# One ring of 8 KB buffers for all weights, and part of the second feed-forward's operand sums made ahead in DRAM

## The chip, the cores and the metric

The kernel runs on one core of one Trainium2 chip, as one launch. The metric is the device time of that launch in microseconds (us); a median over several runs is compared. Five engines work beside each other on the core, each through its own list of instructions, strictly in order: PE (matrix products), DVE (elementwise on vectors), ACT (elementwise, with function tables), POOL and SP. DMAs are issued from SP's queue, some from POOL's and ACT's.

## The reference

One encoder layer on 256 tokens of width 2048, all in float32. What matters here are its two feed-forward blocks, at the start and at the end:

```python
def swiglu(h, w_up, w_down):
    gate, up = jnp.split(h @ w_up, 2, axis=-1)
    return (jax.nn.silu(gate) * up) @ w_down
...
x = x + 0.5 * swiglu(rms_norm(x, ffn1_norm[l]), ffn1_w_up[l], ffn1_w_down[l])
# a gated recurrence, an RG-LRU branch, gates and two projections; then cross-attention
x = x + 0.5 * swiglu(rms_norm(x, ffn2_norm[l]), ffn2_w_up[l], ffn2_w_down[l])
return rms_norm(x, final_norm)
```

The hidden width is 5632, so `w_up` is 2048 x 11264 and `w_down` 5632 x 2048.

## The kernel before

**Precision.** The large products take their operands as `float32r`, each split into a high part `h` (a copy by ACT into that type) and a low part `l` (the difference `raw - h`, by DVE), and each product is made of three matmuls: h·h, l·h and h·l. For every weight piece of 1 MB (128 x 2048 float32, 8 KB in a partition) there is therefore a DMA into `raw`, one pass of ACT and one of DVE before PE can use it.

**Feed-forward.** Each of the two (`ffn1`, `ffn2`) goes through 11 groups `g` of 512 hidden columns. A group has eight up pieces `p` (`wu[g, p]`: two row blocks of the model width, each with 512 gate and 512 up columns), and four down pieces (`wd`) that stand between the groups. `PRODUCTS` names the ways to multiply an up piece with the activations of two token blocks (a 2 x 2 by 2 x 2 block product). "plain" and "mixed" use eight products of blocks, so 8 x 3 = 24 matmuls of 512 columns. "fast" uses seven, so 21 matmuls, in the manner of Strassen; for it four sums of the weight blocks (`td`) are made first, and these are split too, into `th` and `tl`. `ffn_order` says which pieces are of which kind: group 0 is plain; in groups 1 and 2 the even pieces are mixed and the odd ones fast; from g = 3 on only p = 6 is mixed. A down piece takes 24 matmuls.

**Relief for DVE.** Some pieces are of the kind "added" (`begin_added`): ACT writes -h to `l`, and a DMA from POOL's queue adds `raw` (tile `own`) to it, so DVE has no part in it. These are the mixed piece p = 6 of each group from g = 3 on and 16 of the down pieces, in both feed-forwards.

**Buffers.** The 8 KB tiles lie in rings of their own: 3 `raw`, 3 `h`, 3 `l` for the whole program, and within the feed-forwards 3 `wide` (for `td`, `tl`, the eviction tile `ev` and `junk`) and one `own`: 13 in all.

**Order.** Operations are recorded in the order of the code and then arranged by a planner (`Flow.arrange`): it keeps a due time for each operation, prices of the operations and the rings' free buffers, and it writes out for every engine a list in which the instructions stand. The chip follows that list. Between the feed-forwards lies what is called the middle here: 194 pieces, all plain, with the recurrences and the attention beside them.

**Transposes.** When a group's hidden columns are ready, `turn` transposes them on PE (tile names `vt,ev`), two times four transposes, and splits them into `hidop` for the down products.

Of the kernel before, what the change touches and what calls it, by code (L numbers as in the profile page):

```python
# [14 lines left out]
P = 128  # L15
T = 256
# [26 lines left out]
def ffn_order():  # L43

    out, down = [("plain", 0, p) for p in range(8)], [("down", 0, 1, c, 0) for c in range(4)]
    for g in range(1, NG):  # L50
        if g < 3:
            out += [(("mixed", "fast")[p % 2], g, p) for p in (0, 1, 2, 3, 5, 4, 7, 6)]
# [40 lines left out]
class Buffer(View):  # L93


    def __init__(self, ring, shape, dt, name):
        grain = shape[1] if "space" in ring.pool.kw else 1 if shape[1] <= 128 else 32
        super().__init__(self, np.arange(shape[1]) // grain)
        self.ring, self.shape, self.dt, self.name = ring, shape, dt, name
        self.at = self.index = None  # L100
        n = -(-shape[1] // grain)
        self.writer, self.readers = [None] * n, [set() for _ in range(n)]
        self.users = []
        self.left = 0


class Ring:
    def __init__(self, pool, tag, bufs):
        self.pool, self.tag, self.bufs = pool, tag, bufs
        self.takers = []  # L110
        self.spare = bufs if bufs < 8 else bufs // 4
        self.reset()

    def reset(self):
        self.free = [(0.0, i, None) for i in range(self.bufs)]
        self.head, self.taken = 0, set()

    def when(self, op):

        if not self.free or self.takers[self.head] is not op and len(self.free) <= self.spare:  # L120
            return 1e18
        return min(self.free)[0]

    def take(self, op):
        f = min(self.free)
        self.free.remove(f)
# [3 lines left out]
        return f  # L130


class Pool:
# [5 lines left out]
    def tile(self, shape, dt, name, tag=None, bufs=None):  # L139
        tag = tag or name  # L140
        if tag not in self.rings:
            self.rings[tag] = Ring(self, tag, bufs or self.bufs)
        return Buffer(self.rings[tag], shape, dt, name)
# [20 lines left out]
AHEAD, BACKLOG = 30, 3  # L164
# [3 lines left out]
class Flow:  # L168


    def __init__(self, tc):
        self.tc, self.ops, self.pools, self.scopes = tc, [], [], 0
        nc = tc.nc
        self.queues = [Queue(self, n, e) for n, e in (
            ("PE", nc.tensor), ("DVE", nc.vector), ("ACT", nc.scalar), ("SP", nc.sync), ("POOL", nc.gpsimd))]

# [4 lines left out]
    def record(self, queue, method, args, kw):  # L181
# [28 lines left out]
        for v in {v.tile for v in ins + outs}:  # L210
# [5 lines left out]
            s = v.ring.pool.scope  # L216
# [7 lines left out]
    def price(self, op, method, args, kw, outs):  # L224
# [8 lines left out]
        elif q == "PE":  # L233
            op.busy += n / 2400 + 0.0134 if not op.turn else 0.021 if n <= 32 else 0.07 + n * 1.05e-3
# [25 lines left out]
    def arrange(self):  # L260
        from heapq import heappop, heappush
# [15 lines left out]
        for p in self.pools:  # L277
            for r in p.rings.values():
                r.reset()
        live = [0] * (self.scopes + 1)  # L280
# [8 lines left out]
        dma = reached = 0.0  # L289
        events = []  # L290
        for t in {t for op in ops for t in op.tiles}:
            t.left, t.ends = len(t.users), 0.0
        for op in ops:
            if not op.waits:
                cand[op.queue.name].append(op)
# [4 lines left out]
        opened = 0  # L300
        while events:
            t, e = heappop(events)
            if free[e] > t + 1e-9:
                continue
            best, soon = None, 1e18
            for op in cand[e]:
                r = op.ready
                if op.scope is not None and any(live[:op.scope]) and any(x.ring.pool.scope is not None for x in op.takes):
                    continue
                for x in op.takes:  # L310
                    r = max(r, x.ring.when(op))
                if op.nominal > reached + AHEAD:
                    r = 1e18
                if op.moved:
                    r = max(r, dma - BACKLOG)
                if r <= t + 1e-9:
                    if best is None or op.due < best.due:
                        best = op
# [23 lines left out]
            for x in op.takes:  # L342
                f = x.ring.take(op)
                woken.update(names)
                x.index = f[1]
                x.before = f[2]
                if f[2] is not None:
                    for u in f[2].users:
                        if u is not op:
                            u.extra.append(op)  # L350
            if op.scope is not None:
                live[op.scope] -= 1
                if not live[op.scope]:
                    woken.update(names)
            for x in op.tiles:
                x.left -= 1
                x.ends = max(x.ends, op.end)
                if not x.left:
                    x.ring.free.append((x.ends, x.index, x))
                    woken.update(names)  # L360
            for s in op.after:
# [9 lines left out]
                if not s.waits:  # L371
                    cand[s.queue.name].append(s)
# [9 lines left out]
    def emit(self):  # L382
# [13 lines left out]
        for _ in range(3):  # L396
            self.arrange()
        with ExitStack() as outer:
# [3 lines left out]
            for op in self.sequence:  # L402
                if op.scope is not None and op.scope != scope and op.takes:
                    if inner is not None:
                        inner.close()
                    inner, scope = ExitStack(), op.scope
                    open_pools(inner, scope, reuse_waits="tile")
                for x in op.takes:
                    x.at = x.ring.pool.at.tile(x.shape, x.dt, name=x.name, tag=f"{x.ring.tag}{x.index}")
# [6 lines left out]
def block_kernel(tc: tile.TileContext, xT, xin, memT, vec, gfin, bgate, lruw, wu1, wd1, win, wv,  # L416
# [6 lines left out]
    rawp = pool("raw", 3)  # L423
    hp = pool("h", 3)
    lp = pool("l", 3)
    slots = pool("slots", 24)
    small = pool("small", 2)
    psum = pool("psum", 8, space=bass.MemoryType.PSUM)
    scoped = {}

    @contextmanager
    def scope(**pools):
        for name, bufs in pools.items():
            scoped[name] = pool(name, bufs, flow.scopes)
        flow.scopes += 1
        yield
        scoped.clear()

# [36 lines left out]
    def split_tiles():  # L475
        return hp.tile([P, 2048], F32R, name="h", tag="h"), lp.tile([P, 2048], F32R, name="l", tag="l")
# [3 lines left out]
    orders = dict.fromkeys(("ffn1", "ffn2"), ffn_order())  # L480

    def plan_ffn(name, wu, wd):
        for e in orders[name]:
# [4 lines left out]
            if e[0] == "down" and 0 < e[1] < NG - 2 and (e[3] + e[4] - e[1]) % 2 == 0:  # L488
# [9 lines left out]
    plan_ffn("ffn1", wu1, wd1)  # L498
    for hf in range(2):
# [12 lines left out]
    for name, w in (("mv", wvm), ("o", wo)):  # L512
        for g in range(4):
            plan_rows(name, w, g)
    plan_ffn("ffn2", wu2, wd2)
# [4 lines left out]
    def weights(*key):  # L520
        while plan and len(ahead) < 2:
            i = next(planned)
            k, src, kind = plan.pop(0)
            if i < len(head):
# [4 lines left out]
            if i in rest:  # L529
                rest[i]()  # L530
        k, w = ahead.pop(0)
        assert k == key, (k, key)
        return w

    begun = []

    def begin_added(src):

        raw = scoped["own"].tile([P, 2048], F32, name="own", tag="own")
        l = lp.tile([P, 2048], F32R, name="l", tag="l")  # L540
# [5 lines left out]
    def prepare(src, kind, cuts=1):  # L546

        if kind == "added":
            raw, l = begun.pop(0)
            h = hp.tile([P, 2048], F32R, name="h", tag="h")  # L550
            done["high"] = act.activation(h, raw, ACT.Copy).ins
            return h, l
        raw = rawp.tile([P, 2048], F32, name="raw", tag="raw")
        n = 2048 // cuts
        if kind == "plain":
# [4 lines left out]
            return h, l  # L560
        sp.dma_start(raw, src)
        td = scoped["wide"].tile([P, 2048], F32, name="td", tag="wide")
# [6 lines left out]
        th = hp.tile([P, 2048], F32R, name="h", tag="h")  # L569
        tl = scoped["wide"].tile([P, 2048], F32R, name="tl", tag="wide")  # L570
# [120 lines left out]
    FFN_POOLS = dict(wide=3, own=1, third=1)  # L691

    class TokenSquares:
# [5 lines left out]
        def add(self, c, ts=range(2)):  # L699
            for t in ts:  # L700
                if "wide" in scoped:
                    junk = scoped["wide"].tile([P, 2048], F32, name="junk", tag="wide")[:, :512]
# [53 lines left out]
    BOTH = [0, 2, 4]  # L756
    xd = []

    def operand_pairs(src, gain, q, xg, out):

        for a in src:
# [7 lines left out]
            less = None if i else (h[:, 512:768], l[:, 512:768])  # L769
            if 2 * q + i in BOTH:  # L770
                if 2 * q + i == BOTH[0]:
                    xd.append(slot(F32R, "xd"))
                n = 512 * BOTH.index(2 * q + i)
# [3 lines left out]
        def sums(which=((0, "less"), (0, "sums"), (1, "less"), (1, "sums"))):  # L777
            s = slot(name="xs")
            for i, ((h, l), less) in enumerate(out):
# [13 lines left out]
                if (i or 2 * q in BOTH) and (i, "sums") in which:  # L793
                    if not i and len(which) > 1:
# [26 lines left out]
    def ffn(name, pairs, sq, then, begin=(), sums=(), rstds=()):  # L821
# [18 lines left out]
        def turn(g, hid):  # L840
            for y in range(2):
                acc = bank()
                for z in range(2):
                    for t in range(2):
                        pe.transpose(acc[:, z * T + t * P:][:, :P], hid[t][:, (2 * y + z) * P:][:, :P], ident)
                o = slot(F32R, "hidop")
                ov = o.rearrange("p (z s c) -> p z s c", z=2, s=2)
                av = acc.rearrange("p (z c) -> p z c", z=2)
# [12 lines left out]
        for at, e in enumerate(order):  # L861
# [3 lines left out]
            if kind != "down":  # L865
# [3 lines left out]
                for i, (a, b, n) in enumerate(PRODUCTS[kind]):  # L869
# [3 lines left out]
                    own, less = pairs[p]  # L873
                    products.append((accs[n], part(own, a, P) if a >= 0 else part(less, -1 - a, P), part(w[b // 4] if fast else w, b % 4, 512),
# [4 lines left out]
                if ends or last:  # L879
                    if ends or kind == "plain":  # L880
                        ev = scoped["wide"].tile([P, 2048], F32, name="ev", tag="wide")
# [48 lines left out]
    def head_x(p):  # L930
# [7 lines left out]
        sums = operand_pairs([src[:, a:a + 512]], "ffn1_norm", q, xg, out)  # L938
# [164 lines left out]
    def hgrn(hf):  # L1103
# [70 lines left out]
        for pair in range(2):  # L1174
            os, squares = [], []
            for z in range(2):
# [5 lines left out]
                os.append(o)  # L1182
                s = t1("osq")
# [20 lines left out]
    def lru(hf):  # L1204
# [13 lines left out]
        for to, wi, bias in ((r, 0, "ba"), (i, 4, "bx")):  # L1218
            for n in range(4):
                if n % 2 == 0:  # L1220
                    acc = bank()
                o = acc[:, n % 2 * T:][:, :T]
                pe.matmul(o, lw[:, (wi + n) * P:(wi + n + 1) * P], heads(xc)[:, n], start=True, stop=True)
                act.activation(heads(to)[:, n], o, ACT.Sigmoid, bias=col(bias, hf * 4 + n))
# [319 lines left out]
```

## Time and profile before

| | us |
|---|---|
| median of 3 runs | 2437.06 (2436.94 to 2437.98) |
| the profiled execution | 2436.29 |
| its span, first to last instruction | 2434.5 |
| busy within it: PE, DVE, ACT, POOL | 2423.0, 1910.2, 1455.0, 43.9 |

The page of the profile gives an engine's busy time, its share of the span and its instructions. All work is recorded by one helper, so that every instruction has the line L411, and groups are told apart by the names of their tiles: `acc<-h,xh` writes the accumulator from weights `h` and activations `xh`. The time that one matmul stands in the trace (0.39 us) overlaps with the next one's; what it adds is read from start to start in the timeline. The same is done here for DVE, whose instructions overlap at their ends.

### The profile page before, as it was taken

How to read it: one execution, taken by the hardware profiler on the slowest of the kernel's cores; microseconds unless marked ns; L12 is line 12 of the kernel's file. 1: busy time of each engine (PE TensorE's matmuls, PEld its weight loads, DVE VectorE, ACT ScalarE, POOL GpSimd, SP SyncE). 2: the span in 40 equal slices, each digit the busy share in tenths (PEclk: the TensorE clock that was granted, in tenths of full speed). 3: DMA queues.
4: the chain of work that ended last, by engine and by line, in shares of the span. 5: the costliest groups of instructions: out<-in, count | busy, mean ns of one | idle time of the engine just before them, and what ended most of it. 6: DMA issues, size and time to landing. Idle time of an engine off the chain costs nothing.

```text
span 2434.5 us, 30359 instructions
## 1 busy us (share of the span) xinstructions
PE 2423.0 (100%) x12202; PEld 2020.9 (83%) x12202; DVE 1910.2 (78%) x2088; ACT 1455.0 (60%) x1455; POOL 43.9 (2%) x54
## 2 busy tenths in 40 slices
PE   9999999999999999999999999999999999999998
PEld 8888888888888888888888888888888888888886
DVE  7999999999865757667565766656679999999995
ACT  8566666666654443577435644555555666666664
POOL 0000000000000000000000000000000000000000
PEclk9999999999999999999999999999999999999999
DMA  8568888888745544545555555544555888888883
GB/s 297 207 225 260 258 253 252 248 256 259 253 161 191 190 168 168 197 181 203 196 182 198 199 190 177 186 173 156 185 195 204 247 264 254 258 254 256 253 255 139
DMA packets 77613, 526.46 MB, mean 216 GB/s; under 512 B 8609, under 2 KB 8865, under 8 KB 15521
## 3 DMA queue, kind: packets, MB, share of 16 engines
q1 hardware_dynamic: 69840, 473.06, 53.4%
q0 software_dynamic: 6912, 50.33, 10.9%
q8 instruction: 95, 1.56, 0.2%
q10 hardware_dynamic: 720, 1.13, 0.1%
q14 instruction: 46, 0.37, 0.0%
HBM read 472.07 MB, written 2.10 MB: 195 GB/s over the span
## 4 chain that ended last, share of the span: by engine, by line
PE 92%; DVE 5%; issue 1%; ACT 1%; DMA 0%; ACTq 0%; DVEq 0%
PE acc L411 92%; DVE l L411 2%; DVE td L411 2%; DVE tl L411 1%; DVE ev L411 1%; ACT h L411 1%; DVE x L411 0%; DMA own<-wd 0%; PE warm L411 0%; DMA raw<-wu 0%; DVE hidop L411 0%; ACT x L411 0%; ACT junk L411 0%; ACTq L411 0%; ACT ev L411 0%
## 5 line engine op out<-in xcount | busy, mean ns | idle before, releaser
L411 DVE TENSOR_TENSOR l<-raw,h 128x2048 fp32r<-128x2048 f32 (+2 forms) x404 | 828.8, 2055 | 351.4 <-ACT h L411 200.5
L411 ACT ACTIVATE h<-raw 128x2048 fp32r<-128x2048 f32 (+2 forms) x404 | 697.3, 1729 | 533.8 <-PE acc L411 438.8
L411 PE MATMUL acc<-h,xh 128*128 128x512 f32 x1256 | 465.9, 390 | 0.1
L411 PE MATMUL acc<-h,xl 128*128 128x512 f32 x1256 | 445.6, 389 | 0.0
L411 PE MATMUL acc<-h,hidop 128*128 128x512 f32 x1408 | 438.2, 392 | 0.5 <-ACT h L411 0.5
L411 PE MATMUL acc<-h,ops 128*128 128x512 f32 x1664 | 412.2, 392 | 0.0
L411 PE MATMUL acc<-ops,h 128*128 128x512 f32 x1152 | 394.6, 396 | 0.0
L411 ACT ACTIVATE h<-td 128x1024 fp32r<-128x1024 f32 x256 | 265.2, 1054 | 173.7 <-PE acc L411 73.1
L411 PEld LDWEIGHTS acc<-h,ops 128*128 128x128 f32 x1664 | 310.0, 188 | 63.7
L411 DVE TENSOR_TENSOR tl<-td,h 128x1024 fp32r<-128x1024 f32 x256 | 309.8, 1217 | 9.3 <-ACT h L411 9.2
L411 PEld LDWEIGHTS acc<-h,hidop 128*128 128x128 f32 x1408 | 262.6, 188 | 55.1 <-ACT h L411 1.8
L411 PE MATMUL acc<-ops,l 128*128 128x256 f32 x1152 | 279.4, 280 | 0.0
L411 PEld LDWEIGHTS acc<-h,xl 128*128 128x128 f32 x1256 | 235.8, 188 | 49.6
L411 PEld LDWEIGHTS acc<-h,xh 128*128 128x128 f32 x1256 | 235.1, 188 | 49.7 <-DVE hidop L411 0.9
L411 PE MATMUL acc<-l,hidop 128*128 128x512 f32 x704 | 265.5, 389 | 0.0
L411 PEld LDWEIGHTS acc<-ops,h 128*128 128x128 f32 x1152 | 204.0, 188 | 33.7 <-issue 0.4
L411 PEld LDWEIGHTS acc<-ops,l 128*128 128x128 f32 x1152 | 213.1, 188 | 17.0
L411 PE MATMUL acc<-l,ops 128*128 128x512 f32 x832 | 222.0, 390 | 0.0
L411 PE MATMUL acc<-l,xh 128*128 128x512 f32 x744 | 213.0, 389 | 0.0
L411 PEld LDWEIGHTS acc<-l,ops 128*128 128x128 f32 x832 | 155.6, 188 | 32.1
L411 DVE TENSOR_TENSOR td<-raw,td 128x512 f32<-128x512 f32 x256 | 174.8, 683 | 0.8
L411 PE MATMUL acc<-tl,xh 128*128 128x512 f32 x512 | 165.6, 392 | 0.4 <-DVE tl L411 0.4
(169 smaller groups left out, 1914.1 us busy)
## 6 DMA issues: line engine op xcount, KB each, us to landing
raw<-wu SPq DMA_DIRECT2D x156, 1024.0 KB, 6.5
raw<-wd SPq DMA_DIRECT2D x56, 1024.0 KB, 4.8
l<-own POOLq DMA_DIRECT2D x48, 1024.0 KB, 8.5
raw<-win SPq DMA_DIRECT2D x40, 1024.0 KB, 4.8
own<-wd SPq DMA_DIRECT2D x32, 1024.0 KB, 4.8
raw<-wg SPq DMA_DIRECT2D x32, 1024.0 KB, 4.8
own<-wu SPq DMA_DIRECT2D x16, 1024.0 KB, 5.5
raw<-wab SPq DMA_DIRECT2D x16, 1024.0 KB, 4.7
```

The source lines that it names most:

```text
L411: getattr(op.queue.real, method)(*map(real, args), **{k: real(v) for k, v in kw.items()})
```

## The change

Three things are done.

1. **`ffn2` has fewer mixed pieces.** A table `MIXED` gives each feed-forward its own. In `ffn1` nothing changes. In `ffn2` only p = 4 and 6 of groups 1 and 2 stay mixed, and no piece from g = 3 on (the fourth group). So 4 + 8 = 12 pieces of `ffn2` become fast.
2. **The sums of 36 pieces are made ahead.** For the pieces in `MADE` (six in each of groups 1 and 2, p = 0, 4, 7 in each of g = 3 to 10), POOL's queue loads the piece during the middle, DVE makes the four sums in place, and POOL's queue stores them to a DRAM tile `kept`. Later SP loads three quarters of the piece and its 1 MB of sums, and DVE and ACT only split them (kind "made"). No piece of `ffn2` is of the kind "added" any more.
3. **One ring.** The rings of `raw`, `h`, `l`, `wide` and `own` become one ring `big` of 9 buffers for the whole program and 4 more within each feed-forward, so 13 again, and any of these tiles may take any buffer. The planner's rule for taking one changes with it (`fit`), it now prices a change of PE between float32 and float32r work, and prefers to stay in one of them. In three places of the code the recording order is changed to match (`turn` from g = 3 on, the RG-LRU's eight small products, the output products of the recurrence).

```diff
+MIXED = {
+    "ffn1": {1: (0, 2, 4, 6), 3: (6,)},
+    "ffn2": {1: (4, 6), 3: ()},
+}
+MADE = [(g, p) for g in range(1, NG) for p in range(8) if p not in ((4, 6) if g < 3 else (1, 2, 3, 5, 6))]
...
-            out += [("mixed" if p == 6 else "fast", g, p) for p in (1, 3, 0, 6, 4, 2, 5, 7)]
+            out += [("mixed" if p in mixed[3] else "fast", g, p) for p in (1, 3, 0, 6, 4, 2, 5, 7)]
...
-            if e[0] == "down" and 0 < e[1] < NG - 2 and (e[3] + e[4] - e[1]) % 2 == 0:
+            if name == "ffn2" and e[0] == "fast" and e[1:] in MADE:
+                src, kind = (src, e[1:]), "made"
+            if name == "ffn1" and e[0] == "down" and 0 < e[1] < NG - 2 and (e[3] + e[4] - e[1]) % 2 == 0:
                 kind = "added"
...
-    rawp = pool("raw", 3)
-    hp = pool("h", 3)
-    lp = pool("l", 3)
+    flow.share("big", pool("big", 9), 9)
...
-    FFN_POOLS = dict(wide=3, own=1, third=1)
+    FFN_POOLS = dict(more=4, third=1)
...
+    def make_sums(g, p):
+        raw = big("made", F32)
+        r = [raw[:, i * 512:(i + 1) * 512] for i in range(4)]
+        gps.dma_start(raw, wu2[g, p])
+
+        def sums():
+            for o, a, b in ((1, 0, 1), (0, 0, 2), (2, 2, 1), (3, 3, 2)):
+                dve.tensor_tensor(out=r[o], in0=r[a], in1=r[b], op=ALU.subtract)
+            kept = sums_kept[g, p] = dram.tile([P, 2048], F32, name=f"kept{g}_{p}", tag=f"kept{g}_{p}")
+            gps.dma_start(kept, raw)
...
+        if kind == "made":
+            sp.dma_start(raw[:, 512:], src[0][:, 512:])
+            sp.dma_start(td, sums_kept[src[1]])
+            h, l = split_tiles()
+            split(h[:, 512:], l[:, 512:], raw[:, 512:])
+            th, tl = big("h"), big("tl")
+            split(th, tl, td)
+            return (h, l), (th, tl)
...
+            if e == "PE":
+                busy += 0.1 * (op.turn != last)
+                last = op.turn
...
+            for f, y in ((over, 0), (over, 1), (split_turned, 0), (split_turned, 1)) if g > 2 else (
+                    (over, 0), (split_turned, 0), (over, 1), (split_turned, 1)):
+                f(y)
```

Three places show what this does to the engines' lists. First DVE's list in the second feed-forward, from a late group's transposed hidden columns (`hidop`) on, before:

```order
L411 TENSOR_TENSOR hidop<-acc,hidop 128x2x256 x2
L411 TENSOR_TENSOR td<-raw 128x1024
L411 TENSOR_TENSOR tl<-td,h 128x1024
L411 SCALAR_TENSOR_TENSOR x_424<-acc,x_424 128x512
L411 TENSOR_TENSOR td<-raw,td 128x512
L411 TENSOR_TENSOR l<-raw,h 128x1536
L411 TENSOR_TENSOR td<-raw,td 128x512
L411 SCALAR_TENSOR_TENSOR x_424<-acc,x_424 128x512
L411 TENSOR_TENSOR tl<-td,h 128x1024 x2
L411 TENSOR_TENSOR td<-raw 128x1024
L411 TENSOR_TENSOR l<-raw,h 128x1536
```

The same engine and place in the changed kernel (`x_362` is a residual tile, as `x_424` is):

```order
L464 TENSOR_TENSOR hidop<-acc,hidop 128x2x256 x2
L464 TENSOR_TENSOR td<-raw 128x1024
L464 SCALAR_TENSOR_TENSOR x_362<-acc,x_362 128x512
L464 TENSOR_TENSOR td<-raw,td 128x512
L464 TENSOR_TENSOR l<-raw,h 128x1536
L464 TENSOR_TENSOR td<-raw,td 128x512
L464 TENSOR_TENSOR tl<-td,h 128x1024
L464 TENSOR_TENSOR l<-raw,h 128x1536
L464 TENSOR_TENSOR tl<-td,h 128x1024
L464 SCALAR_TENSOR_TENSOR x_362<-acc,x_362 128x512
L464 TENSOR_TENSOR tl<-td,h 128x2048
L464 TENSOR_TENSOR td<-raw 128x1024
```

Each fast piece has three `td`, one `l` of 1536 and two `tl` of 1024 before; a made piece now stands among them with an `l` of 1536 and one `tl` of 2048, and no `td`.

Second, DVE's list in the middle, in the key projection of the attention (`sum` and `ops` turn a product into the next operand), before:

```order
L411 TENSOR_TENSOR l<-raw,h 128x2048
L411 TENSOR_TENSOR sum<-acc,lo 128x256
L411 TENSOR_TENSOR sum<-sum,rstd 128x256
L411 TENSOR_TENSOR ops<-sum,ops 128x256
L411 TENSOR_TENSOR l<-raw,h 128x2048
```

and in the changed kernel, where `made` is a piece whose sums are made in place:

```order
L464 TENSOR_TENSOR l<-raw,h 128x2048
L464 TENSOR_TENSOR made<-made 128x512 x3
L464 TENSOR_TENSOR sum<-acc,lo 128x256
L464 TENSOR_TENSOR made<-made 128x512
L464 TENSOR_TENSOR sum<-sum,rstd 128x256
```

The four subtractions of a made piece stand between the operands of the middle's products, behind the DMA that loads the piece.

Third, SP's list of DMAs in the second feed-forward, a stretch of one group, before:

```order
L411 DMA own<-wd 128x2048
L411 DMA raw<-wu 128x2048 x3
L411 DMA own<-wu 128x2048
L411 DMA raw<-wu 128x2048 x2
L411 DMA own<-wd 128x2048
L411 DMA raw<-wu 128x2048 x2
L411 DMA raw<-wd 128x2048 x2
```

and in the changed kernel:

```order
L464 DMA raw<-wu 128x2048 x2
L464 DMA raw<-wu 128x1536
L464 DMA td<-kept_0_9919 128x2048
L464 DMA raw<-wu 128x2048
L464 DMA raw<-wu 128x1536
L464 DMA td<-kept_4_10105 128x2048
L464 DMA raw<-wu 128x2048 x2
L464 DMA raw<-wu 128x1536
L464 DMA td<-kept_7_10262 128x2048
L464 DMA raw<-wd 128x2048 x4
```

The loads into `own` are gone, each made piece has two loads in place of one, and all four down pieces go the plain way.

More of the change, by code (lines that the diff above doesn't have):

```diff
@@ L304, in arrange @@
                 continue
+            while later[e] and later[e][0][0] <= reached + AHEAD:
+                enter(heappop(later[e])[2])
             best, soon = None, 1e18
             for op in cand[e]:
+                if best is not None and (not last or best.turn or op.due - STICK > best.due):
+                    break
+                if best is not None and not op.turn:
+                    continue
                 r = op.ready
[L308 to L313, printed above, removed]
                 if op.moved:
@@ L316, in arrange @@
                 if r <= t + 1e-9:
-                    if best is None or op.due < best.due:
-                        best = op
+                    for ring in {x.ring for x in op.takes}:
+                        fit = ring.fit(op, self)
+                        r = max(r, fit[-1][0] if fit else 1e18)
+                if r <= t + 1e-9:
+                    best = op
                 else:
```

233 lines of the change are left out of this document (151 added, 82 removed).

## The prediction

> **What bounds the kernel now.** I read the page first, then the stretches, then the timelines of PE and DVE in the last feed-forward. The page's head and its chain of waits:
>
> ```profile
> span 2434.5 us, 30359 instructions
> PE 2423.0 (100%) x12202; PEld 2020.9 (83%) x12202; DVE 1910.2 (78%) x2088; ACT 1455.0 (60%) x1455; POOL 43.9 (2%) x54
> PE 92%; DVE 5%; issue 1%; ACT 1%; DMA 0%; ACTq 0%; DVEq 0%
> ```
>
> PE is busy from end to end and carries the chain. So the time is PE's work, and every matmul taken out counts, as long as nothing else comes late in its place. What could is seen in the busy time by stretch, the middle first and then `ffn2` without its start and end:
>
> ```profile
> core 0: us, PE busy (x) PEld busy (x) DVE busy (x) ACT busy (x) POOL busy (x), PEclk, DMA share, GB/s
> 720.00:1740.00 1020.00, 1020.00 (x5901) 862.75 (x5900) 652.34 (x759) 533.07 (x622) 0.96 (x1) 1.00 0.52 184
> 1860.00:2340.00 480.00, 479.61 (x2140) 394.60 (x2139) 452.51 (x460) 323.30 (x262) 19.08 (x22) 1.00 0.81 253
> ```
>
> In the middle DVE is busy for 652 of 1020 us. In `ffn2` it is busy for 452.5 of 480 us, 94%: right behind PE. ACT (323) and the DMA engines (0.81) have room. How close the two are shows where PE waits for DVE; the middle columns are start, time in the trace, and idle time before with its releaser:
>
> ```profile
> 2150.92 0.74 PE L411 MATMUL acc<-tl,xh 128*128 128x512 f32 x2 [0.39 <-DVE tl L411]
> 2152.86 1.52 PE L411 MATMUL acc<-l,xh 128*128 128x512 f32 x6
> ...
> 2154.22 0.39 PE L411 MATMUL acc<-h,xh 128*128 128x512 f32 x1
> ```
>
> Six matmuls take 2154.22 - 2152.86 = 1.36 us, so one adds 0.227 us. The first row is a wait for the low part of a fast piece's sums. The next rows show one place of five groups in a row, the first block of transposes, and for one of the groups also what follows it:
>
> ```profile
> 2066.85 0.60 PE L411 MATMUL acc<-vt,ev 128*128 128x128 f32 x4
> 2128.58 0.60 PE L411 MATMUL acc<-vt,ev 128*128 128x128 f32 x4
> 2190.94 0.60 PE L411 MATMUL acc<-vt,ev 128*128 128x128 f32 x4
> 2191.29 0.48 PE L411 MATMUL acc<-h,hidop 128*128 128x512 f32 x1
> 2191.61 0.60 PE L411 MATMUL acc<-vt,ev 128*128 128x128 f32 x4
> 2191.97 1.40 PE L411 MATMUL acc<-h,hidop 128*128 128x512 f32 x5
> 2252.53 0.60 PE L411 MATMUL acc<-vt,ev 128*128 128x128 f32 x4
> 2314.29 0.60 PE L411 MATMUL acc<-vt,ev 128*128 128x128 f32 x4
> ```
>
> The groups take 61.73, 62.36, 61.59 and 61.76 us, 61.86 in the mean. The best, 61.59, is PE's own pace; 0.27 us a group is lost to waits.
>
> **1. Matmuls.** Twelve pieces of `ffn2` go from eight products to seven, three matmuls each: 36 x 0.227 = **-8.2 us**. All of it is PE's time. Four of these pieces (-2.7 us) lie in groups 1 and 2, eight (-5.4 us) in g = 3 to 10.
>
> **2. Fewer changes of PE between kinds of work.** In the lists of PE the visits to float32 work go from 100 to 76. Fourteen are pairs of four transposes joined to eight. Two blocks of four with a matmul between take 2191.97 - 2190.94 = 1.03 us, without that matmul (0.227) 0.80; eight in a row take as long:
>
> ```profile
> 663.28 1.03 PE L411 MATMUL acc<-vt,x 128*128 128x128 f32 x8
> 664.07 1.62 PE L411 MATMUL acc<-h,hidop 128*128 128x512 f32 x6
> ...
> 1073.32 0.58 PE L411 MATMUL acc<-h,ops 128*128 128x512 f32 x1
> 1073.74 0.66 PE L411 MATMUL acc<-xc,lw 128*128 128x256 f32 x2
> ```
>
> 664.07 - 663.28 = 0.79, so joining transposes brings nothing. The RG-LRU's small products (`xc,lw`) are joined too, six visits fewer: there one matmul between two visits takes 0.42 us instead of 0.227. At most 6 x 0.19 = 1.1 is saved, at least nothing; I take half: **-0.6 us**. The other four joined visits I leave at nothing.
>
> **3. DVE in `ffn2`, g = 3 to 10.** What one DVE instruction adds, from start to start:
>
> ```profile
> 2152.05 1.23 DVE L411 TENSOR_TENSOR tl<-td,h 128x1024 fp32r<-128x1024 f32 x1 [0.58 <-ACT h L411]
> 2153.19 1.22 DVE L411 TENSOR_TENSOR td<-raw 128x1024 f32<-128x1024 f32 x1
> 2154.33 1.22 DVE L411 TENSOR_TENSOR tl<-td,h 128x1024 fp32r<-128x1024 f32 x1
> 2155.46 0.69 DVE L411 TENSOR_TENSOR td<-raw,td 128x512 f32<-128x512 f32 x1
> 2156.06 1.75 DVE L411 TENSOR_TENSOR l<-raw,h 128x1536 fp32r<-128x1536 f32 x1
> 2157.73 0.68 DVE L411 TENSOR_TENSOR td<-raw,td 128x512 f32<-128x512 f32 x1
> ...
> 2174.10 2.29 DVE L411 TENSOR_TENSOR l<-raw,h 128x2048 fp32r<-128x2048 f32 x1 [1.99 <-ACT h L411]
> 2176.31 1.22 DVE L411 TENSOR_TENSOR tl<-td,h 128x1024 fp32r<-128x1024 f32 x1
> ...
> 2187.49 0.74 DVE L411 SCALAR_TENSOR_TENSOR ev<-ev,rtok 128x512 f32<-128x512 f32 x1
> 2188.15 0.68 DVE L411 SCALAR_TENSOR_TENSOR x<-acc,x 128x512 f32<-128x512 f32 x1
> 2188.75 0.68 DVE L411 TENSOR_TENSOR td<-raw,td 128x512 f32<-128x512 f32 x1
> ```
>
> So 2048 elements add 2.21, 1536 1.67, 1024 1.14, 512 0.60, the scaling of `ev` 0.66. A fast piece costs DVE 1.14 + 2 x 0.60 + 1.67 + 2 x 1.13 = 6.27; a made one 1.67 + 2.21 = 3.88; a down piece 2.21; a group's evictions, residuals and `hidop` 13 x 0.60 + 2 x 0.66 = 9.1. Before, a group has 7 fast, 2 plain down pieces and the evictions (one mixed and two down pieces are added by POOL's DMA): 43.9 + 4.4 + 9.1 = 57.4 us on DVE, against PE's 61.59. After, 5 fast, 3 made, 4 plain down: 31.4 + 11.6 + 8.8 + 9.1 = **60.9 us**, against PE's 61.59 - 3 x 0.227 = **60.9**. The two are level: DVE's four spare microseconds are gone. It stays just fast enough, and comes into g = 3 with as much lead as 13 buffers hold, because groups 1 and 2 (six made pieces each) leave it idle.
>
> What that costs is seen in no row. Below: the 0.27 lost now may vanish, since one ring lets DVE run ahead with any buffer: -2.2 over eight groups. Above: with DVE level, each stop of DVE is a stop of PE. The nearest row is the 0.58 us that DVE stood before `tl` waiting for ACT; two of these per group are +1.16 - 0.27, so +7.1. I take 0.4 lost per group instead of 0.27, near the present loss, since that arises at single points where PE catches up with DVE, though DVE's total leaves 4 us; the points stay and the reserve behind them goes: **+1.0 us**.
>
> **4. The middle.** DVE gets 36 x 4 subtractions of 512: 144 x 0.60 = 86 us, and is then busy for 738 of 1020 us. The 72 DMAs of 1 MB are paid from these rows:
>
> ```profile
> q1 hardware_dynamic: 69840, 473.06, 53.4%
> l<-own POOLq DMA_DIRECT2D x48, 1024.0 KB, 8.5
> raw<-wab SPq DMA_DIRECT2D x16, 1024.0 KB, 4.7
> DMA to landing us min/median/max: 4.6/7.7/12.3
> ```
>
> 0.534 x 2434.5 us for 473 MB is 2.9 us of all DMA engines for 1.05 MB; 72 x 2.9 = 208 us raise the share from 0.52 to 0.72. Both are covered by PE. In order, the subtractions wait for POOL's load, and the middle's `l`, `sum` and `ops` are queued behind them. No row shows a plain load from POOL: its neighbours are 4.7 us by SP and 8.5 with an add, the slowest of tile `own` 12.3 (last row). [...] If a load came 12.3 - 4.7 = 7.6 us late, DVE would stand that long, once in 194 / 36 = 5.4 pieces. Against that:
>
> ```profile
> 1162.23 2.29 DVE L411 TENSOR_TENSOR l<-raw,h 128x2048 fp32r<-128x2048 f32 x1 [3.20 <-ACT h L411]
> 1167.67 2.29 DVE L411 TENSOR_TENSOR l<-raw,h 128x2048 fp32r<-128x2048 f32 x1 [3.15 <-ACT h L411]
> ```
>
> DVE stands idle 3.2 of the 5.44 us of each piece, for a buffer, and a finished piece lies ahead: 3.2 + 5.4 = 8.6 us of cover, won back over the next three pieces. **0**, ends 0 and +2.4 (one block of four subtractions once ahead of something that PE awaits).
>
> **5. At nothing:** the removed `own` passes of ACT (ACT has a third of its time free) and POOL's 24 adding DMAs; the shared ring in `ffn1`, where the work is the same.
>
> **Sum.** -8.2 - 0.6 + 1.0 + 0 = -7.8. The profiled execution took 2436.29 us; the median of the runs, 2437.06, is 0.8 above. So 2428.5 as profiled, **2429.3** as the median.
>
> **Rivals.**
> - *DVE stops twice a group* (chance 0.13). For it: two stops of 0.58 behind ACT now go unseen because of DVE's slack. A group takes 60.9 + 1.16 = 62.1, 0.2 above today's 61.86; over eight groups +1.6, with -2.7 from groups 1 and 2 and -0.6: 2435.4, no change that counts. Against it: ACT is busy for two thirds only.
> - *DVE becomes the bound and stops at every second pair of `h` and `l`* (0.08): the three made pieces wait for two loads each, and one late DMA now stops PE. Four stops a group, 60.9 + 2.3 = 63.2, are 1.36 x 8 = +10.9 - 3.3 = +7.6: 2444.7, slower. It decides from 61.86 + 3.3 / 8 = 62.3 us a group on, that is 1.4 us of stops. Against it: the DMA share falls there, from 12 loads and 3 adds to 14.25 loads.
> - *DVE pays the time that its instructions stand in the trace* (0.02): 2.29, 1.75, 1.22, 0.68 and 0.74 us instead of the spacings. A group then has 5 x 6.77 + 3 x 4.04 + 4 x 2.29 + 13 x 0.68 + 2 x 0.74 = 65.4, +3.5 x 8 - 3.3 = +25: 2462. The rows above speak against it, since starts follow closer. [...]
> - *Late loads in the middle outlast the cover* (0.02): 36 x 1 us, 2465.
>
> That the matmuls are not fewer is no rival: the lists show it.
>
> **Forecast and chances.** What is left, 0.75, goes to the forecast. Its own range is 8.2 + 1.1 + 2.2 below (2425.6) to 2432. The range for eight in ten leaves out the corner where all the small gains come together and the three slow cases, and takes in the first rival: 2427.0 to 2435.8. About 0.2% (4.9 us) is what a measurement of this kernel can tell from no change: faster than 2432.2 0.75, within 0.13, slower 0.12.
>
> **What would show it.** Right: PE's groups in `ffn2` about 60.9 to 61.3 us apart, DVE busy above 98% there, PE not idle in the middle, `made` loads landing under 13 us. Wrong: groups at 62 us or more with PE idle behind `tl` or `l` (step 3), or PE idle between 720 and 1740 us (step 4).

## The result, and the profile after

| | before | after |
|---|---|---|
| median, us | 2437.22 (4 runs, 2436.94 to 2437.98) | 2451.91 (4 runs, 2450.3 to 2456.57) |
| profiled execution, us | 2436.29 | 2456.57 |
| its span, us | 2434.5 | 2454.8 |

The ratio after to before is 1.0063, 95% interval 1.005 to 1.0076: slower by 0.6%, where 0.3% faster was forecast. The head of the page after:

```profile
span 2454.8 us, 30751 instructions
...
PE 2423.6 (99%) x12166; PEld 2018.0 (82%) x12166; DVE 2010.7 (82%) x2171; ACT 1405.8 (57%) x1408; POOL 61.7 (3%) x102
```

PE runs the 36 matmuls fewer that were promised (12202 to 12166), and yet it is busy no less: 2423.6 us, and the span is 20 us longer. Busy time by stretch after, the same two stretches and columns as in the prediction (the last three are granted clock, DMA share and GB/s):

```profile
720.00:1740.00 1020.00, 1003.95 (x5795) 847.05 (x5794) 713.16 (x860) 504.02 (x595) 35.32 (x65) 0.99 0.67 246
1860.00:2340.00 480.00, 478.55 (x2133) 392.15 (x2132) 474.74 (x423) 293.92 (x233) 0.00 (x0) 1.00 0.67 247
```

In `ffn2` PE is busy for 478.55 of 480 us, nearly as before (479.61), with DVE up from 452.51 to 474.74: the two are close to each other, and PE stands for little over 1 us. In the middle PE was busy for all of the 1020 us and now stands for 16 of them, at a mean clock of 0.99. The loss is there. The groups of `ffn2`, read at the first transposes of five groups in a row:

```profile
2090.39 1.03 PE L464 MATMUL acc<-vt,ev 128*128 128x128 f32 x8
...
2151.90 1.03 PE L464 MATMUL acc<-vt,ev 128*128 128x128 f32 x8
...
2213.03 1.03 PE L464 MATMUL acc<-vt,ev 128*128 128x128 f32 x8
...
2274.32 1.03 PE L464 MATMUL acc<-vt,ev 128*128 128x128 f32 x8
...
2335.34 1.03 PE L464 MATMUL acc<-vt,ev 128*128 128x128 f32 x8
```

They are 61.51, 61.13, 61.29 and 61.02 us apart, 61.24 in the mean, where 61.3 was forecast and 61.86 stood before. So one looks at the middle for the places where PE stands. The largest, in the timeline of three engines after (rows of other engines and of PE left out between):

```profile
923.03 1.42 DVE L464 TENSOR_TENSOR made<-made 128x512 f32<-128x512 f32 x2 [2.94 <-DMA made<-wu]
...
926.96 0.63 DVE L464 TENSOR_TENSOR made<-made 128x512 f32<-128x512 f32 x1
...
928.00 0.54 POOL L464 DMA_DIRECT2D kept<-made  x1 [11.93 <-DVE ya L464]
...
931.31 0.42 DVE L464 TENSOR_TENSOR plain<-plain,rstd 128x256 f32<-128x256 f32 x1
...
937.35 4.49 DVE L464 TENSOR_TENSOR l<-raw,h 128x2048 fp32r<-128x2048 f32 x2 [5.61 <-DMA kept<-made]
...
939.69 0.58 PE L464 MATMUL acc<-ops,l 128*128 128x256 f32 x1 [5.55 <-DVE l L464]
```

These six rows show the largest stop from end to end. DVE stands 2.94 us for the load of a made piece, makes the sums, POOL issues the store at 928.00. The next `l` has nothing to do with that piece, but it was given the buffer of the `made` tile, and so DVE stands 5.61 us until the store has landed, and goes on 9.35 us after its issue. PE waits 5.55 us for that `l`. The second largest stop, 2.56 us at 1401 us, has the same two waits of DVE ahead of it (2.59 us for the load, 1.55 us for the store). Not every stop is of this form: the next three (1.56 and 1.59 us at 1210 us, 1.45 us at 1584 us) follow weight loads that landed late, for which ACT had stood 7.14 and 4.66 us. No row shows how much of these goes back to the made pieces; the run without making, below, has none of the five. The view of waits after, where such rows are added up (engine and tile, releaser: sum in us, times, longest), the rows of the DMAs with their median from issue to landing, and the landing of tile `kept`'s transfers:

```profile
DVE made L464 <- DMA made<-wu: 32.6, 15, 4.3
...
DVE l L464 <- DMA kept<-made: 18.8, 8, 5.6
...
made<-wu POOLq DMA_DIRECT2D x36, 1024.0 KB, 5.2
kept<-made POOLq DMA_DIRECT2D x36, 1024.0 KB, 6.2
...
DMA to landing us min/median/max: 4.1/6.5/11.8
```

The planner prices each at 0.9 + 2.9 + 1.9 = 5.7 us, more where it reckons with other transfers still ahead, and takes the buffer as free then. In the trace 13 of the 36 loads and 22 of the 36 stores land later than 5.7 us after their issue, the longest load after 9.3 us and the longest store after 11.8. SP's list, too, stands for stores, 17 times and 89.6 us in all, since weight tiles take over such buffers as well.

### The profile page after: what moved, and what is told of

Its sections match the earlier page's. It is cut to its first block, busy times and chain, and to the rows that moved or that the text cites. A ratio compares the mean times of both kernels' runs of the same rounds, so it can differ in the third digit from the quotient of the medians.

```text
span 2454.8 us, 30751 instructions
## 1 busy us (share of the span) xinstructions
PE 2423.6 (99%) x12166; PEld 2018.0 (82%) x12166; DVE 2010.7 (82%) x2171; ACT 1405.8 (57%) x1408; POOL 61.7 (3%) x102
## 3 DMA queue, kind: packets, MB, share of 16 engines
q8 instruction: 95, 1.56, 0.2%
## 5 line engine op out<-in xcount | busy, mean ns | idle before, releaser
L464 DVE TENSOR_TENSOR l<-raw,h 128x2048 fp32r<-128x2048 f32 (+2 forms) x428 | 875.7, 2051 | 226.3 <-ACT h L464 115.8
L464 ACT ACTIVATE h<-raw 128x2048 fp32r<-128x2048 f32 (+2 forms) x428 | 736.6, 1725 | 536.0 <-PE acc L464 145.1
L464 ACT ACTIVATE h<-td 128x1024 fp32r<-128x1024 f32 (+1 forms) x244 | 286.8, 1182 | 208.3 <-DVE td L464 182.8
L464 DVE TENSOR_TENSOR tl<-td,h 128x1024 fp32r<-128x1024 f32 (+1 forms) x244 | 333.0, 1373 | 22.1 <-ACT h L464 14.4
L464 PE MATMUL acc<-ops,l 128*128 128x256 f32 x1152 | 273.6, 282 | 8.1 <-DVE l L464 8.1
L464 PE MATMUL acc<-l,xh 128*128 128x512 f32 x688 | 198.8, 390 | 0.0
L464 PE MATMUL acc<-tl,xh 128*128 128x512 f32 x560 | 174.3, 391 | 0.3 <-DVE tl L464 0.2
L464 PEld LDWEIGHTS acc<-l,hidop 128*128 128x128 f32 x704 | 132.2, 188 | 27.4
```

Source lines behind the costliest of these rows:

```text
L464: getattr(op.queue.real, method)(*map(real, args), **{k: real(v) for k, v in kw.items()})
```

## The experiments

**Theory.** In the one ring a weight tile takes over the buffer of a `made` tile at the moment at which the planner believes the store has landed. Many of the loads and most of the stores land later than their price; DVE, in order, stands before the sums and again before the next `l`, and PE follows. **Rivals:** DVE's 86 us of extra sums; the extra DMA traffic; the ring and the new order by themselves; an unlucky order. Each edit makes the planner write a new order, so a control with a harmless edit is among the runs. The kernel before stood at 2437.14 to 2437.24 us beside each of these runs.

**1. Parts of the making left out.** These three kernels do not compute the reference's result for the 36 pieces. Without making (the second feed-forward loads raw pieces in the place of the sums):

```diff
-            make_ahead(i - between[0])
...
-            sp.dma_start(td, sums_kept[src[1]])
+            sp.dma_start(td, src[0])
```

> No sums are made in the middle; the second feed-forward loads its td tiles straight from the raw weight pieces, so the same bytes are loaded there, split and multiplied, but the result of those 36 pieces is not the reference's. One ring, the planner's new rules, 36 matmuls fewer and the second feed-forward stay. Theory (the made tiles in the shared ring cost the loss, and the prediction's other steps were right): about 2429 us, the prediction's own number. Rival 'extra DVE work' and rival 'extra DMA traffic': also 2429 to 2431. Rival 'the ring and the planner's order cost it': 2445 to 2452, with the PE gaps between 900 and 1700 us still there.

Measured: 2431.99 us, ratio to before 0.9978 (0.9969 to 0.9988). The rival of the ring and the order falls: without the making the kernel is 5 us faster than before, so the making costs 20 us, more than the whole loss. The 3 us that are missing to the forecast (2429.3) lie elsewhere. Without the store only:

```diff
-            kept = sums_kept[g, p] = dram.tile([P, 2048], F32, name=f"kept{g}_{p}", tag=f"kept{g}_{p}")
-            gps.dma_start(kept, raw)
```

> The made pieces are loaded and their sums made in the middle, but not stored; td is loaded from the raw weights, so the result of 36 pieces is not the reference's. Theory (a made tile holds its buffer of the shared ring from the load to the landing of the store, and the next l or raw waits for it): the waits of l for the store (18.8 us of DVE) and of SP (89.6 us) go, about two thirds of the 22 us, 2436 us (2432 to 2441). Rival 'DVE's 86 us of sums': 2452, no change. Rival 'late loads alone stop DVE in order': 2450. Rival 'DMA traffic': half of it is gone, 2440.

Measured: 2433.68 (0.9981, 0.9972 to 0.9991). DVE makes all 144 sums here, and 18 of the 20 us that making costs are gone: the rival of DVE's work falls. Late loads alone do not stop PE either: DVE stands 45.3 us for them in this kernel (32.6 in the changed one), and PE is busy for 1018 of the middle's 1020 us. Without the sums only:

```diff
-            for o, a, b in ((1, 0, 1), (0, 0, 2), (2, 2, 1), (3, 3, 2)):
-                dve.tensor_tensor(out=r[o], in0=r[a], in1=r[b], op=ALU.subtract)
```

> The made pieces are loaded and stored again, but DVE makes no sums: the 144 subtractions are left out. Theory (holding of the buffer by load and store): the buffer is held about 2.4 us less, DVE no longer stands before sums whose load is late; about half of the loss stays, 2440 to 2446. Rival 'DVE's work in order': 2429 to 2432. Rival 'DMA traffic': 2450.

Measured: 2435.62 (0.9994, 0.9985 to 1.0004). All 72 DMAs are there, and 16 us are gone: the rival of the traffic falls. The theory's own number (2440 to 2446) was too high. The parts don't add: each taken out alone removes most of the loss, so the stops need load, sums and store together.

**2. The buffer.** All the work, but the made tile in a buffer of its own, whose 8 KB come from two of the 24 `slots`:

```diff
-        raw = big("made", F32)
+        raw = scoped["mk"].tile([P, 2048], F32, name="made", tag="made")
...
-    slots = pool("slots", 24)
+    slots = pool("slots", 22)
...
-    middle.enter_context(scope(tmp=8, tmp2=2, scores=1, extra=2, feature=3))
+    middle.enter_context(scope(tmp=8, tmp2=2, scores=1, extra=2, feature=3, mk=1))
```

> The made tile gets a buffer of its own in the middle (8 KB, taken from two of the 24 slots); nine buffers stay for raw, h and l, and the result is the reference's. Theory: no weight tile waits for a store any more, PE's gaps between 900 and 1700 us fall from about 25 to 10 us, 2433 to 2437. Rival 'DVE's work' and rival 'late loads stop DVE': 2448 to 2452. Rival 'DMA traffic': 2450. With two slots fewer, a wait for a slot may cost up to 3 us.

Measured: 2434.91 (0.9993, 0.9984 to 1.0003). The same loads, sums and stores cost 17 us less. In the waits of this kernel the store's landing now stops only the next load on POOL, and DVE stands for such a load only once:

```profile
POOL made L464 <- DMA kept<-made: 216.2, 35, 11.0
...
DVE made L464 <- DMA made<-wu: 5.5, 1, 5.5
```

**3. The price.** The ring as in the changed kernel, one number of the planner changed:

```diff
             op.moved = n * 512 / 2 ** 20 * (5.2 if "accum_op" in kw else 2.9)
+            op.late = 4.0 if q == "POOL" and "accum_op" not in kw else 0.0
...
-                op.end = dma + 1.9
+                op.end = dma + 1.9 + op.late
```

> The changed kernel, only the planner believes that a plain DMA from POOL's queue lands 4 us later than it did (5.7 us before, the trace has 6.2 us in the median and 11.8 at most for the stores). Theory (the planner hands on a made tile's buffer at a time at which the store has not landed, and DVE and SP stand in order behind it): it then hands on another buffer or later, 2433 to 2440. Rival 'nine buffers are too few for weights and made tiles, whatever the plan': 2446 to 2455.

Measured: 2432.56 (0.9982, 0.9972 to 0.9991), 19 us below the changed kernel and slightly better than expected, so nine buffers are enough. Its waits:

```profile
POOL made L465 <- DMA kept<-made: 24.9, 4, 8.7
...
DVE made L465 <- DMA made<-wu: 11.1, 2, 7.9
```

No `l` waits for a store any more. The opposite dose, -2.0 in place of 4.0:

> The opposite dose: the planner believes that POOL's plain DMAs land 2 us earlier than it did. Theory: the buffers are handed on still earlier, more and longer stops, 2455 to 2480. Rival 'unlucky draw': 2430 to 2440.

Measured: 2492.96 (1.0236, 1.0214 to 1.0257), 41 us above the changed kernel; one number of the planner moves the time by 60 us between its two ends. Its waits, against 32.6 and 18.8 in the changed kernel:

```profile
DVE made L465 <- DMA made<-wu: 103.4, 26, 7.7
...
ACT h L465 <- DMA kept<-made: 43.4, 10, 9.1
...
DVE l L465 <- DMA kept<-made: 13.4, 4, 4.7
```

The control, `"ACT": 0.18` in place of 0.16 in the planner's `LAG`:

> A control: the changed kernel with the planner's lag behind an ACT instruction at 0.18 us in place of 0.16, which rearranges many instructions but says nothing of POOL's DMAs. Theory (a wrong price makes the planner place stops again and again): still slow, 2444 to 2456. Rival 'the changed kernel's order was one unlucky draw, and any other is good': 2430 to 2437.

Measured: 2448.89 (1.0048, 1.0033 to 1.0063). The loss is there again, with the same stop at the same place:

```profile
928.13 0.54 POOL L464 DMA_DIRECT2D kept<-made  x1 [12.06 <-DVE ya L464]
...
938.04 4.49 DVE L464 TENSOR_TENSOR l<-raw,h 128x2048 fp32r<-128x2048 f32 x2 [6.17 <-DMA kept<-made]
```

As a control this is weak: some nine tenths of DVE's list in the middle stand in the same succession as in the changed kernel, about six tenths with the later price. What speaks against an unlucky draw is the series: 2492.96 with the price 2 us lower, 2451.91 and 2448.89 as it was, 2432.56 and 2432.41 (below) with 4 and 8 us more, and the waits go with it. The later price for the stores alone, then for the loads alone:

> As the run with the later landing, but only the stores (kept from made) are priced 4 us later in the planner, not the loads. Theory (it is the store's landing that gives the buffer free too late): all or nearly all of the gain, 2432 to 2436. Rival 'DVE stands in order before a late load': 2445 to 2452.

> As the run with the later landing, but only the loads of the made pieces are priced 4 us later, not the stores. Theory (the store): most of the loss stays, 2445 to 2452. Rival 'late loads': 2432 to 2436. If both are needed for a long stop, as the runs without sums and without stores hint, it falls between, near 2440.

Measured: 2436.84 (0.9998, 0.9989 to 1.0008) and 2434.11 (0.9988, 0.9978 to 0.9997). The second was not expected: the theory with the store alone had 2445 to 2452. The waits of the two kernels, stores and then loads priced later:

```profile
DVE made L465 <- DMA made<-wu: 35.0, 17, 4.2
DVE l L465 <- DMA kept<-made: 1.2, 1, 1.2
...
DVE l L465 <- DMA kept<-made: 12.8, 7, 4.2
ACT h L465 <- DMA kept<-made: 5.4, 1, 5.4
DVE made L465 <- DMA made<-wu: 4.4, 2, 3.5
```

Each mends its own wait and leaves most of the other, and in both PE is busy for 1018.6 to 1019.0 of the middle's 1020 us. So neither wait alone reaches PE; the long stops need both, as under 1. With 8 us in place of 4:

> As the run with the later landing, with 8 us in place of 4. Theory (the price only has to cover the real landing, 11.8 us at most against 5.7 + 4): 2431.5 to 2434, no difference from 4. Rival 'the later the better': 2430 or below. Rival 'too late a price takes buffers from the weights and shifts sums into the second feed-forward's start': 2435 to 2440.

Measured: 2432.41 (0.9982, 0.9973 to 0.9991), no different from 4. Here neither DVE nor ACT waits for the load of a made piece or for its store, and PE is busy in the middle as it was before the change:

```profile
720.00:1740.00 1020.00, 1019.58 (x5897) 862.35 (x5896) 730.72 (x883) 516.62 (x612) 35.67 (x66) 1.00 0.68 251
```

Own buffer and price together:

> The made tile in a buffer of its own and the planner's later landing of POOL's plain DMAs (4 us more), both. Theory: the own buffer has already taken the waits for the store away, and the price keeps DVE from standing before a late load: 2432 to 2434.5 beside 2434.9 with the own buffer alone. Rival 'what is left in the middle is DVE's own chains': 2435, no difference. If the price makes the planner put sums at worse places: 2436 to 2440.

Measured: 2436.35 (0.9994, 0.9985 to 1.0004): nothing is gained by doing both, against the theory's 2432 to 2434.5. Whether the sums stand at worse places there was not looked into.

**4. The prediction's other terms.** The ring alone (no making, the kinds of `ffn2` as before):

```diff
-    "ffn2": {1: (4, 6), 3: ()},
+    "ffn2": {1: (0, 2, 4, 6), 3: (6,)},
...
-MADE = [(g, p) for g in range(1, NG) for p in range(8) if p not in ((4, 6) if g < 3 else (1, 2, 3, 5, 6))]
+MADE = [(g, p) for g in range(1, NG) for p in range(8) if p < 0]
...
-            if name == "ffn1" and e[0] == "down" and 0 < e[1] < NG - 2 and (e[3] + e[4] - e[1]) % 2 == 0:
+            if e[0] == "down" and 0 < e[1] < NG - 2 and (e[3] + e[4] - e[1]) % 2 == 0:
```

> One ring and the planner's new rules, the joined transposes, but no sums made ahead and the second feed-forward's pieces of the same kinds as before (mixed and added), so 36 matmuls more than in the changed kernel; the result is the reference's. By the prediction's steps 2 and 5 (joined work saves 0.6 us, the ring costs nothing): 2436.5 us beside 2437.1 of the kernel before. Rival 'the ring costs what the run without making fell short of the prediction': 2439 to 2440. Against the run without making (2432.0) the 36 matmuls of step 1 should show as +8.2 us less what step 3 costs: 2439 to 2440 by step 1 alone.

Measured: 2437.87 (1.0002, 0.9992 to 1.0011), the same as before. From here to the run without making, 5.9 us are gained by the 36 matmuls fewer and what comes with them, where steps 1 and 3 have 7.2. The groups of `ffn2` in this kernel:

```profile
2070.18 1.03 PE L464 MATMUL acc<-vt,ev 128*128 128x128 f32 x8
...
2254.42 1.03 PE L464 MATMUL acc<-vt,ev 128*128 128x128 f32 x8
```

Three groups in 184.24 us are 61.41 each, below the 61.59 that the prediction took for PE's own pace.

**5. How much of a late DVE is covered.** On the kernel with the later price, for five pieces of the middle:

```diff
+                for _ in range(STALL.get(next(plains), 0)):
+                    dve.tensor_tensor(out=raw, in0=raw, in1=raw, op=ALU.max)
+                    flow.ops[-1].busy = 0.07
```

> The kernel with the later landing (2432.6), and at five of the middle's weight pieces DVE passes 4, 5, 6, 8 and 10 times over the raw tile first (maximum with itself, the values stay), 2.21 us each, which the planner is told cost 0.07 us: DVE is 8.8, 11.1, 13.3, 17.7 and 22.1 us late. By the prediction's cover of 8.6 us PE stops for 0.2, 2.5, 4.7, 9.1 and 13.5 us, 30 us in all, and if PE goes on at its pace, 2463. If after a stop of over 3.5 us PE runs at half pace for some 4 us, as behind the stop at 933 us, 2 us more for each of three: 2469. If the cover is only the 3.2 us that DVE stood for a buffer, 57 us of stops and 2 us each: 2495 to 2500.

Measured: 2492.47 (1.0227, 1.0207 to 1.0247), 60 us above the kernel that it is made from. Three of the forced delays on DVE, and the matmuls that stood for the last two:

```profile
742.80 9.26 DVE L465 TENSOR_TENSOR raw<-raw 128x2048 f32<-128x2048 f32 x4
...
1414.47 18.57 DVE L465 TENSOR_TENSOR raw<-raw 128x2048 f32<-128x2048 f32 x8 [0.67 <-DMA raw<-wq]
...
1435.04 1.22 PE L465 MATMUL acc<-ops,h 128*128 128x512 f32 x2 [15.60 <-ACT h L465]
...
1521.11 23.22 DVE L465 TENSOR_TENSOR raw<-raw 128x2048 f32<-128x2048 f32 x10
...
1546.38 1.22 PE L465 MATMUL acc<-ops,h 128*128 128x512 f32 x2 [18.61 <-ACT h L465]
```

Passes in place follow each other 2.3 us apart, so the delays are 9.26, 11.6, 13.9, 18.57 and 23.22 us. From start to start beyond its usual pace PE lost nothing at the first, 6.0 and 5.2 us (in three pieces) at the next two, and 15.6 and 18.6 us in the query and key projections. The cover of 8.6 us that the prediction used holds at the first and the third (9 us and more, 8.7) and not at the second (5.6); in the projections it is 3.0 and 4.6. Of the forecasts the one with the cover of 3.2 us and a slower pace after each stop (2495 to 2500) came nearest.

**6. Fewer mixed pieces still.** With the own buffer, then with the later price, also p = 4 and 6 of groups 1 and 2 fast:

```diff
-    "ffn2": {1: (4, 6), 3: ()},
+    "ffn2": {1: (), 3: ()},
...
-MADE = [(g, p) for g in range(1, NG) for p in range(8) if p not in ((4, 6) if g < 3 else (1, 2, 3, 5, 6))]
+MADE = [(g, p) for g in range(1, NG) for p in range(8) if p not in (() if g < 3 else (1, 2, 3, 5, 6))]
```

> The made tile in a buffer of its own, and also p = 4 and 6 of groups 1 and 2 of the second feed-forward by seven products, their sums made ahead too (40 pieces in all); the result is the reference's. Theory (PE's matmuls set the time while DVE is fed): 4 x 3 x 0.227 = 2.7 us less than with the own buffer alone, 2432.2. Rival 'at the start of the second feed-forward DVE has no lead and PE waits for th and tl there': 2434 to 2438.

> The later landing by 4 us in the planner, and p = 4 and 6 of groups 1 and 2 of the second feed-forward by seven products too (40 pieces made ahead); the result is the reference's. Theory: 12 matmuls fewer, 2.7 us below 2432.6, 2429.9. Rival 'the second feed-forward's start has no room for DVE', as with the own buffer, where groups 1 and 2 lost it again: 2433 to 2437.

Measured: 2438.02 (1.0004, 0.9994 to 1.0013) and 2439.95 (1.0016, 1.0007 to 1.0026), each some us above the kernel with the mixed pieces. With the later price PE stops at 1806 to 1926 us, in the first groups of `ffn2`, for `h` and `l`, as the rival said. With the own buffer its largest stop (3.4 us) lies at 1360 us, in the middle, so that run bears on the rival only in part.

## Why the prediction was wrong, step by step

**Step 4, the middle, is the one that failed.** It was put at 0, with ends 0 and +2.4, and cost about 20 us: 2451.91 against 2431.99 without the making. Three things in it were wrong. It asked only whether a late *load* would be covered; the *store* and the buffer that it holds were counted as DMA time and as nothing else, though in one shared ring the next owner of that buffer waits for the store to land. It took the cover from two pieces at 1162 us, in the gate products, and spread it over the middle; in the projections the forced stops found 3.0 and 4.6 us in place of 8.6. The largest stop shows both at once: before it DVE stood 2.94 + 5.61 = 8.55 us beside the four sums (2.4 us), of which a cover of 8.6 us leaves 2.4 at most, and PE stopped for 5.55. And it asked how long a load takes to land, but not what the planner believes, on which the order rests: that price, 5.7 us, stands in the code. The loads themselves landed within 9.3 us, inside the 13 that the prediction named as a sign of being right. (The middle has 176 pieces, not 194, one made piece in 4.9; nothing turns on that.)

The rival nearest to it, late loads that outlast the cover, had a chance of 0.02 and 36 stops of 1 us. There were fewer and longer ones, and 20 us came of them in place of 36; late loads alone, as it has them, did no harm (under 1). In the changed kernel the middle has five stops of PE of over 1.4 us, the largest of 5.55; PE stands for 16 us there in all, and some 4 us more are a slower pace behind two places with stops (last section).

**Steps 1 and 3 came out near their number, in part by luck.** The groups at 61.24 us are 0.62 shorter than before, by 0.68 for the matmuls less 0.06; the forecast was +0.13 for the second. But with the ring and the joined transposes alone they stand at 61.41, so PE's pace without the three matmuls is 60.73 and 0.5 us a group is lost beside DVE, where 0.4 was forecast from a pace of 60.9. The start of `ffn2` was taken as free, and is not quite: from its first group's transposes to the fourth's the run without making takes 156.3 us in place of 157.7, with 14 matmuls (3.2 us) fewer, so it lost some 2 us there, and the runs under 6 show how little room there is.

**Steps 2 and 5** can't be told apart here, and the -0.6 of step 2 can't be seen: with the ring and the joined work alone the time is within 0.9992 and 1.0011 of before. That is a sum, though: the groups of `ffn2` are shorter there by about 0.2 us each, and in the one trace the stretch from the last transposes of `ffn1` to the first of `ffn2` is 1142.6 us in place of 1140.7. Which part of the change brings the one and which the other wasn't tested.

With the price mended the change does most of what it was forecast to do: 2432.4 and 2432.6 against 2429.3. The run without any making, 2432.0, lacks the last 3 us too, so they don't lie in the making; some 2 of them are the start of `ffn2`, the rest stays open.

## What to carry to other kernels

When a tile moves into a shared ring, look up who takes its buffer next and what frees it: a store frees it when it lands, not when it is issued (9.35 us later at the largest stop here), and the waiter is whoever comes next in order, not whoever reads the data. When an order is written out ahead by a planner, compare its prices with the landing times in the trace, the late ones and not the median, and err to the late side: here a price 8 us higher cost nothing, and one 2 us lower cost 41 us more. Cover is to be read at the tightest stretch, not at the nearest.

## What the runs showed of the hardware

PE ran slower behind some of its stops. Granted clock by stretch in the changed kernel (the column behind the last busy time), at two of its stops:

```profile
900.00:960.00 60.00, 54.45 (x461) 46.89 (x462) 44.24 (x52) 21.94 (x24) 2.56 (x4) 0.94 0.54 187
1200.00:1260.00 60.00, 56.85 (x252) 46.65 (x251) 40.41 (x38) 22.88 (x15) 2.14 (x4) 0.97 0.69 260
```

Before the change both stretches are at 1.00. At the stop of 5.55 us, from 934 us on, the record of the granted clock shows half speed for 6.8 us, part of which still falls into the stop:

```profile
938.00:944.50 6.50, 4.81 (x16) 4.23 (x17) 6.50 (x4) 1.91 (x1) 0.00 (x0) 0.50 0.41 161
```

A matmul of 512 columns takes 0.43 us from start to start there in place of 0.23. Behind the two stops of 1.56 and 1.59 us at 1211 and 1213 us the record shows half speed for 3.4 us, from 1214.4 us on, and 16 matmuls take 5.33 us there (1214.04 to 1219.37) in place of 16 x 0.227 = 3.63. The stop of 2.56 us at 1401 us has no such stretch: from 1380 to 1440 us the clock stands at 1.00. The run with the forced delays (under 5), in the stretches around its stops of 5.84, 2.97, 15.60 and 18.61 us:

```profile
1020.00:1040.00 20.00, 14.16 (x56) 11.49 (x55) 17.76 (x15) 6.73 (x9) 0.53 (x1) 0.83 0.53 185
1120.00:1140.00 20.00, 17.03 (x64) 13.51 (x62) 14.57 (x9) 9.79 (x13) 0.53 (x1) 0.83 0.31 109
1410.00:1450.00 40.00, 24.40 (x130) 20.99 (x129) 34.96 (x31) 11.35 (x16) 1.06 (x2) 0.79 0.44 160
1520.00:1560.00 40.00, 21.39 (x111) 18.39 (x110) 37.74 (x27) 9.62 (x11) 1.07 (x2) 0.74 0.30 111
```

Taken as half speed, that is an estimated 6.8, 6.8, 16.8 and 20.8 us (twice the missing clock times the stretch), part of it in the stops themselves. Behind the stop, by the starts of the matmuls, the slower pace cost 3.1, 2.9, 1.7 and 2.4 us in this order, and 2.5 and 1.7 us at the two places of the changed kernel: no more after 19 us than after 3. So the stop of 2.97 us cost about twice itself. The 3.5 us of the expectation, from which on a stop was to bring the slower pace, were its author's assumption; the stop of 2.97 us brought it, too.

Transfers of 1 MB from POOL's queue landed 5.2 us (load) and 6.2 us (store) after their issue in the median of the changed kernel. What stopped DVE were single landings such as the one of 9.3 us at 928 us, which a median doesn't tell.
